# Decoder block: the operands of the down projection are made during gate/up and stored, and gate/up's products accumulate in PSUM

## The chip, the cores and the metric

One core of one Trainium2 chip. The metric is the device time of one execution in microseconds (us), less is better. All data is float32.

## The reference

One layer of a decoder trunk for 1024 tokens of width 1024. The part that matters here is the feed-forward block, with d_ff = 2816:

```python
x = x + merged @ w_out[i]
h = rms_norm(x, norm_ffn[i])
x = x + (jax.nn.silu(h @ w_ffn_gate[i]) * (h @ w_ffn_up[i])) @ w_ffn_down[i]
gate = jax.nn.sigmoid(rms_norm(x, norm_ple[i]) @ w_ple_gate[i])
```

Ahead of it come an input projection, a pooling mixer and an attention, after it an embedding gate and a final norm. None of those is changed.

## The kernel before

Features lie on the 128 partitions, tokens run along the free dimension. TensorE multiplies float32r operands, so each float32 operand is held as a pair hi + lo, made by `split`: ScalarE casts hi (L105), VectorE subtracts it for lo (L106). A product of two pairs takes three matmuls (`mm3`, L85 to L87), each 128x128 by 128x512.

Gate, up and down each use Strassen's scheme in Winograd's form: seven products in place of eight, for a pair of 128 outputs, two halves of the contracted features and two halves of the tokens. One such group is called a strassen here.

**Gate and up.** For each of 11 pairs of output tiles one strassen of gate and one of up run in turn (`strassen`). Each has 7 products of 12 matmuls, so 84. A product goes to a PSUM bank of its own (`bank`, eight of them, in turn). GpSimd sums the four weight pieces (L688 to L691), each weight operand is split, and the seven activation operands (`b11` to `t4`) have been made once ahead. Results are combined on VectorE: p1 is copied out by ScalarE (L682), and six adds from PSUM (`plus`, L674; one of p5 is used twice, so seven instructions) form the four outputs. Gate's outputs pass Silu (L712); up's are multiplied with them (L723) and written to DRAM (`d_a`, `flush`, L719), as plain float32. The order of each engine's instructions here is found by the framework's list scheduler, not by the program text; weight casts run three products ahead of TensorE (`bufs=4`).

**Down.** It runs over five chunks of four feature tiles and, in each, four pairs of output tiles (`mp`): 20 strassens of 7 products of 6 matmuls, 168 matmuls a chunk. The order is written by hand (`manual_schedule`). For the next chunk, `staged` loads eight activation tiles from `d_a` (L760), and `building` makes its 14 operands: 8 subtractions on GpSimd (L782, L788, L793, L798) and 14 splits, of which 12 subtract on VectorE and 2 on GpSimd (`LATE`). `prepare` makes the next strassen's weight operands (GpSimd L851 to L854, then splits: three of 512 columns, one of 256). `evacuate` adds each product from PSUM to a sum (L868 on ScalarE for 16 products of the first chunk, L870 on VectorE for the rest). In the last chunk nothing is built; `combine` forms x from the sums on GpSimd and VectorE (L879). The building of chunk 0 happens beside the last up strassen.

Operands lie in a ring of 48 tiles of 128x512 in three pools (`tap`, `tbp`, `spare`).

Of the kernel before, what the change touches and what calls it, by code (L numbers as in the profile page):

```python
# [16 lines left out]
P = 128  # L17
S = 1024
# [20 lines left out]
LATE = (("t3", 2), ("t4", 2))       # operands of down whose low parts GpSimd makes  # L39
# [6 lines left out]
def hybrid_block(ctx, tc, xT, pT, gains, pscale, w_u, w_qk, w_v, w_ga, w_gb, w_pool, w_a, w_b,  # L46
# [36 lines left out]
    def mm3(ps, w, x, first, last):  # L83
        """ps += (w_hi + w_lo)^T (x_hi + x_lo), less lo^T lo."""
        nc.tensor.matmul(ps, w[0], x[0], start=first, stop=False)  # L85
        nc.tensor.matmul(ps, w[0], x[1], start=False, stop=False)  # L86
        nc.tensor.matmul(ps, w[1], x[0], start=False, stop=last)  # L87
# [25 lines left out]
    def inv_rms(ps, acc, n, y):  # L113
        """y: [128 tokens, n], 1 / rms of n tiles of tokens; acc: sums of squares [features, n * 128]."""
        for t in range(n):
            nc.tensor.matmul(ps[:, t:t + 1], acc[:, t * P:(t + 1) * P], ones[:, :1], start=True, stop=True)
        a = const.tile([P, KT], F32, name="nrm_a", bufs=2)[:, :n]
        t = const.tile([P, KT], F32, name="nrm_t", bufs=2)[:, :n]
        nc.vector.tensor_scalar(a, ps[:, :n], EPS, None, ALU.add)
        # the first guess from the exponent's bits (within 4%), then Newton's steps  # L120
        nc.vector.tensor_scalar(y.bitcast(I32), a.bitcast(I32), -0.5, float(0x5f3759df), ALU.mult, ALU.add)
        for _ in range(3):
            nc.vector.tensor_mul(t, a, y)
            nc.vector.scalar_tensor_tensor(t, t, -0.5, y, ALU.mult, ALU.mult)
            nc.vector.scalar_tensor_tensor(y, t, 1.5, y, ALU.add, ALU.mult)
# [5 lines left out]
    def stat(psp, acc, n, diag):  # L131
        """diag: 1 / rms of n tiles of tokens, as diagonals side by side."""
# [5 lines left out]
    def spread(psp, diag, n):  # L138
        """[128, n * 128] in PSUM: the diagonals' entries along the free dimension, on all partitions."""
# [7 lines left out]
    def move(dst, src):  # L147
        """float32r as it is, through scratch in DRAM."""
# [28 lines left out]
    # x: load, times the norm's gain, split; the first three column tiles of u as x comes in  # L177
# [62 lines left out]
    def to_qk(pool, psp, i):  # L240
        """i < 4: q of a pair of heads; else k."""
# [17 lines left out]
    # pooling mixer  # L259
# [41 lines left out]
    # v: [keys, heads, 128]; hi|lo for even heads, lo|hi for odd ones  # L301
# [80 lines left out]
    with att, pool("att", 2) as ap, ExitStack() as pss:  # L382
# [5 lines left out]
        def scores(ld, qt):  # L388
            """The weights of 128 queries over the keys, [queries, keys]."""
# [31 lines left out]
        def turn(b, qt, ats):  # L421
            """[keys, queries], split; of a pair's two tiles, the second starts one block of keys later."""
# [23 lines left out]
        def att_out(h, hh, av):  # L446
            """hi part of v on the head's own half, lo part on the other."""
# [81 lines left out]
    # weights from here on, in pieces of 512 columns  # L529
# [23 lines left out]
    # [128, 512] operands: three pools, filled in turn, 16 + 24 + 8 tiles, as one ring  # L553
    def operand_tile(pool, dt=F32R):
        return pool.tile([P, HALF], dt, name="t")

    def operand(pool, n=4):
        return [(operand_tile(pool), operand_tile(pool)) for _ in range(n)]

    sparex = ctx.enter_context(ExitStack())  # L560
    spare = sparex.enter_context(pool("spare", 8, side="right"))
# [22 lines left out]
    tap = ctx.enter_context(pool("tap", 16))  # L584
# [75 lines left out]
    tbp = tbx.enter_context(pool("tbp", 24, side="right"))  # L660
    t2, t1, b22 = (operand(tbp) for _ in range(3))
    tb2x = ctx.enter_context(ExitStack())
    tb2 = tb2x.enter_context(pool("tb2", 16))
    t3, t4 = operand(tb2), operand(tb2)

    def product(a, b, k0=0):
        ps = bank()
        for k in range(len(b)):
            mm3(ps, col(a, k0 + k), b[k], k == 0, k == len(b) - 1)
        return ps  # L670

    def plus(ps, t, into=None):
        into = ev() if into is None else into
        nc.vector.tensor_add(into, ps, t)  # L674
        return into

    def strassen(src, out):
        """out(e, h, t): e-th tile of 128 outputs, half h of the tokens; a step is one product."""
        a11, a12, a21, a22 = (piece(src[e][:, hs(c)]) for e in range(2) for c in range(2))
        p1 = product(halves(a11), b11)  # L680
        t = ev()
        nc.scalar.copy(t, p1)  # L682
        yield
        p2 = product(halves(a12), b21)
        out(0, 0, plus(p2, t))
# [18 lines left out]
        yield  # L704
        p4 = product(halves(a22), t4)
        out(1, 0, plus(p4, t, t))
# [4 lines left out]
    def gate_out(e, h, t):  # L711
        nc.scalar.activation(t, t, AF.Silu)  # L712
# [4 lines left out]
    def flush(n):  # L717
        for _ in range(min(n, len(writes))):
            nc.sync.dma_start(*writes.pop(0))  # L719

    def up_out(i):
        def f(e, h, t):
            nc.vector.tensor_mul(t, t, gated.pop((e, h)))  # L723
            writes.append((d_a[2 * i + e][:, hs(h)], t))
        return f

# [25 lines left out]
    # down: the same products, over pairs of 128 outputs and four tiles of features at a time  # L752
    def staged(c, tile):
        """Activations of a chunk, k-th tiles of its halves: [k][y11, y12, y22, y21]."""
        ys = []
        for k in range(2):
            ys.append([])
            for f, h in ((k, 0), (k, 1), (2 + k, 1), (2 + k, 0)):
                ys[-1].append(tile())
                nc.sync.dma_start(ys[-1][-1], d_a[4 * c + f][:, hs(h)])  # L760
                yield ys

    ring = {"at": 0}

    def ring_pair():
        pair = []
        for _ in range(2):
            i = ring["at"] % 48
            ring["at"] += 1
            pair.append(operand_tile(tap if i < 16 else tbp if i < 40 else spare))  # L770
        return tuple(pair)

    def building(ys, o):
        """The chunk's operands in the order of the ring; a step is one of them, split."""
        for y in ys:
            o["b11"].append(ring_pair())
            split(*o["b11"][-1], y[0], teng("b11", len(o["b11"])))
            yield
        for y in ys:
            o["b21"].append(ring_pair())  # L780
            split(*o["b21"][-1], y[3], teng("b21", len(o["b21"])))
            nc.gpsimd.tensor_sub(y[0], y[1], y[0])  # L782
            yield
        t2s = [ring_pair() for _ in ys]
        for y in ys:
            o["t1"].append(ring_pair())
            split(*o["t1"][-1], y[0], teng("t1", len(o["t1"])))
            nc.gpsimd.tensor_sub(y[0], y[2], y[0])  # L788
            yield
        for y, t in zip(ys, t2s):  # L790
            o["t2"].append(t)
            split(*t, y[0], teng("t2", len(o["t2"])))
            nc.gpsimd.tensor_sub(y[1], y[2], y[1])  # L793
            yield
        for y in ys:
            o["b22"].append(ring_pair())
            split(*o["b22"][-1], y[2], teng("b22", len(o["b22"])))
            nc.gpsimd.tensor_sub(y[3], y[3], y[0])  # L798
            yield
        for n, i in (("t3", 1), ("t4", 3)):  # L800
            for y in ys:
                o[n].append(ring_pair())
                split(*o[n][-1], y[i], teng(n, len(o[n])))
                yield

    def operands():
        return {n: [] for n in ("b11", "b21", "t2", "t1", "b22", "t3", "t4")}

    def teng(n, k):
# [279 lines left out]
```

## Time and profile before

| what | value |
|---|---|
| runs | 1490.47, 1491.53, 2020.46 us; median 1491.53 |
| span of the profiled execution | 1489.5 us |
| TensorE busy | 1430.5 us, 96% |
| VectorE busy | 1075.6 us, 72% |
| ScalarE busy | 618.6 us, 42% |
| GpSimd busy | 479.8 us, 32% |
| DMA | 174.54 MB, mean 117 GB/s |

The profile is of one execution, whose own time outside the span is not listed; the two undisturbed runs lie 1.0 and 2.0 us above its span. A matmul's listed duration overlaps the next one's, so a matmul's cost is read from the distance between starts, or from a stretch's length over its count.

### The profile page before, as it was taken

To read this page: it belongs to the slowest core of one execution; us is meant where nothing else is said; L and a number is where in the kernel's file an instruction comes from. 1 tells how busy PE (TensorE), PEld (TensorE's weight loads), DVE (VectorE), ACT (ScalarE), POOL (GpSimd) and SP (SyncE) were. 2 spreads that over 40 slices of the span, in tenths; PEclk is the share of its full clock that TensorE was granted. 3 is DMA by queue.
4 is the path that set the end of the run, shared out by engine and by line. 5 is a ranking of instruction groups with operands and counts; after the bars stand their busy time and mean duration, and the time that the engine had idled before them with its cause. 6 is when DMAs were issued, how large, how long until landed. Compare 5 with 4: busy or idle time off the path is not lost.

```text
span 1489.5 us, 19114 instructions
## 1 busy us (share of the span) xinstructions
PE 1430.5 (96%) x6538; PEld 1172.3 (79%) x6538; DVE 1075.6 (72%) x1634; ACT 618.6 (42%) x1146; POOL 479.8 (32%) x501
## 2 busy tenths in 40 slices
PE   8999999999999999998999999999999999987995
PEld 7888888888888878886888888888877777765885
DVE  7671268888777786679655555555579899999786
ACT  6131455555555443446333333333335433325443
POOL 5000022333232200016323222232356676779001
PEclk9999999999999999999999999999999999998998
DMA  5140874555442187332332222222224333211452
GB/s 198 64 140 24 278 215 142 154 157 143 128 127 72 50 272 237 114 119 87 117 121 86 79 83 80 80 83 73 84 64 135 114 99 113 71 43 57 134 178 70
DMA packets 94032, 174.54 MB, mean 117 GB/s; under 512 B 9968, under 2 KB 21744, under 8 KB 93936
## 3 DMA queue, kind: packets, MB, share of 16 engines
q1 hardware_dynamic: 93936, 173.33, 36.7%
q8 instruction: 51, 0.84, 0.2%
q14 instruction: 45, 0.37, 0.1%
HBM read 128.21 MB, written 45.09 MB: 116 GB/s over the span
## 4 chain that ended last, share of the span: by engine, by line
PE 74%; DVE 11%; issue 8%; POOL 4%; ACT 1%; DMA 1%; SPq 0%; POOLq 0%; DVEq 0%; ACTq 0%
PE mm L87 23%; PE mm L86 23%; PE mm L85 23%; DVE wlo L106 2%; DVE t L106 2%; DVE fail L410 1%; PE pt L428 1%; DVE xsl L110 1%; PE av L444 1%; PE av L443 1%; PE z L400 1%; PE z L401 1%; POOL x L879 1%; DVE s L870 1%; DVE x L957 1%
## 5 line engine op out<-in xcount | busy, mean ns | idle before, releaser
L105 ACT CAST whi<-wraw 128x512 fp32r<-128x512 f32 x336 | 206.2, 621 | 488.9 <-PE mm L86 357.0
L87 PE MATMUL mm<-t,wlo 128*128 128x512 f32 x960 | 381.2, 397 | 12.1 <-DVE wlo L106 12.0
L85 PE MATMUL mm<-t,whi 128*128 128x512 f32 x960 | 380.5, 397 | 12.0 <-ACT whi L105 8.3
L86 PE MATMUL mm<-t,whi 128*128 128x512 f32 x960 | 379.4, 395 | 1.2 <-DVE t L106 1.2
L106 DVE TENSOR_TENSOR wlo<-wraw,whi 128x512 fp32r<-128x512 f32 x336 | 264.4, 792 | 124.1 <-ACT whi L105 124.1
L87 PEld LDWEIGHTS mm<-t,wlo 128*128 128x128 f32 x960 | 181.9, 189 | 61.0 <-DVE wlo L106 20.7
L85 PEld LDWEIGHTS mm<-t,whi 128*128 128x128 f32 x960 | 181.9, 190 | 55.9 <-ACT whi L105 10.6
L86 PEld LDWEIGHTS mm<-t,whi 128*128 128x128 f32 x960 | 181.7, 189 | 43.4 <-DVE t L106 2.2
L674 DVE TENSOR_TENSOR ev<-mm,ev 128x512 f32<-128x512 f32 x154 | 106.0, 689 | 128.3 <-PE mm L87 126.6
L85 PE MATMUL mm<-xs,whi 128*128 128x512 f32 x384 | 154.6, 403 | 0.0
L87 PE MATMUL mm<-xs,wlo 128*128 128x512 f32 x384 | 150.4, 392 | 0.0
L86 PE MATMUL mm<-xs,whi 128*128 128x512 f32 x384 | 150.2, 391 | 0.0
L688 POOL TENSOR_TENSOR ws<-wraw 128x512 f32<-128x512 f32 x22 | 30.7, 1397 | 329.5 <-DMA wraw<-in_w_gate 224.2
L410 DVE TENSOR_TENSOR_SCAN fail<-fail 128x1024 f32<-128x1024 f32 (+3 forms) x64 | 87.3, 1364 | 27.3 <-POOL fail L408 26.8
L408 POOL TENSOR_SCALAR_AFFINE_SELECT fail<-fail 128x128 f32<-128x128 f32 x64 | 20.5, 320 | 227.0 <-ACT fail L406 200.5
L87 PEld LDWEIGHTS mm<-xs,wlo 128*128 128x128 f32 x384 | 72.1, 188 | 15.8
L105 ACT CAST ath<-pt 128x256 fp32r<-128x256 f32 (+1 forms) x176 | 54.8, 335 | 69.0 <-PE pt L428 38.9
L85 PEld LDWEIGHTS mm<-xs,whi 128*128 128x128 f32 x384 | 72.2, 188 | 11.9 <-ACT sg L372 0.2
L86 PEld LDWEIGHTS mm<-xs,whi 128*128 128x128 f32 x384 | 72.4, 188 | 11.5
L106 DVE TENSOR_TENSOR t<-ev,t 128x512 fp32r<-128x512 f32 x76 | 78.3, 1043 | 0.4
L106 DVE TENSOR_TENSOR atl<-pt,ath 128x256 fp32r<-128x256 f32 (+1 forms) x176 | 61.4, 367 | 18.2 <-ACT ath L105 17.9
L409 POOL TENSOR_SCALAR_AFFINE_SELECT beta<-beta 128x128 f32<-128x128 f32 x64 | 66.5, 1038 | 22.6 <-ACT beta L407 21.0
(191 smaller groups left out, 2608.2 us busy)
## 6 DMA issues: line engine op xcount, KB each, us to landing
wraw<-in_w_gate SPq DMA_DIRECT2D x44, 256.0 KB, 2.6
wraw<-in_w_up SPq DMA_DIRECT2D x44, 256.0 KB, 2.6
d_a<-ev SPq DMA_DIRECT2D x44, 256.0 KB, 2.0
wraw<-in_w_down SPq DMA_DIRECT2D x44, 256.0 KB, 2.7
ev<-d_a SPq DMA_DIRECT2D x36, 256.0 KB, 4.3
wraw<-in_w_out SPq DMA_DIRECT2D x32, 256.0 KB, 3.1
wraw<-in_w_pg SPq DMA_DIRECT2D x32, 256.0 KB, 2.6
wraw<-in_w_qk SPq DMA_DIRECT2D x8, 512.0 KB, 4.6
```

What stands on the lines that cost most here:

```text
L85: nc.tensor.matmul(ps, w[0], x[0], start=first, stop=False)
L86: nc.tensor.matmul(ps, w[0], x[1], start=False, stop=False)
L87: nc.tensor.matmul(ps, w[1], x[0], start=False, stop=last)
L105: nc.scalar.copy(hi, src)
L106: (eng or nc.vector).tensor_sub(lo, src, hi)
L110: nc.vector.scalar_tensor_tensor(lo, src, g, hi, ALU.mult, ALU.subtract)
L400: nc.tensor.matmul(zo, q[:, base:base + P], kh[:, ks], start=True, stop=False)
L408: nc.gpsimd.affine_select(r[:, :P], r[:, :P], [[1, P]], ALU.is_gt, 1.0, base=0, channel_multiplier=-1)
L409: nc.gpsimd.affine_select(b[:, :P], b[:, :P], [[1, P]], ALU.is_gt, 0.0, base=0, channel_multiplier=-1)
L410: nc.vector.tensor_tensor_scan(r[:, :w], r[:, :w], r[:, :w], 1.0, ALU.mult, ALU.bypass)
L674: nc.vector.tensor_add(into, ps, t)
L688: nc.gpsimd.tensor_add(s1, a21, a22)
```

## The change

Gate/up: p1, p6, p7 and p4 of a strassen now accumulate in one PSUM bank (`x`) and p5 and p3 in a second one (`y`); p2 has its own. Between two products on the same bank its content is read: ScalarE copies p1, p1+p6 (`u2`) and p5 out (three copies in place of one), and VectorE adds for three outputs (three adds in place of seven). The fourth output needs no add. p7 and p3 change places.

After each up strassen (but the last) its four outputs stay in SBUF. `stage` makes from them the seven operands of down during the next gate strassen: 7 splits (ScalarE and VectorE) and 4 subtractions on GpSimd, one step behind each product. Each operand, hi and lo side by side in one 128x1024 tile of `spare`, is written to DRAM (`d_o`, 512 KB each, 70 in all), on the same queue as the weight loads.

Down: `staged` and `building` are gone. `loading` fetches 14 operands of 512 KB per chunk, straight into the ring (now 24 tiles of 128x1024); chunk 0's are fetched during the last up strassen. To pair the tiles rightly, `prepare` takes even and odd feature tiles as the two halves, so its operands are strided views. Matmuls, evacuations and `combine` stay as they were.

```diff
-    d_a = [scr(f"d_a{i}", [P, S]) for i in range(FT)]
+    d_o = [{n: scr(f"d_{n}{i}", [P, S]) for n in DOWN} for i in range(FT // 2 - 1)]
...
+        def kept(ps):
+            t = ev()
+            nc.scalar.copy(t, ps)
+            return t
+
+        x = product(halves(a11), b11)
+        p1 = kept(x)
+        yield
+        out(0, 0, product(halves(a12), b21), p1)
         yield
...
-        p6 = product(halves(a11), t2)
-        plus(p6, t, t)
-        yield
-        p5 = product(halves(s1), t1)
-        c12 = plus(p5, t)
-        yield
-        p3 = product(halves(a12), b22)
-        out(0, 1, plus(p3, c12, c12))
-        yield
-        p7 = product(halves(a21), t3)
-        plus(p7, t, t)
-        out(1, 1, plus(p5, t))
-        yield
-        p4 = product(halves(a22), t4)
-        out(1, 0, plus(p4, t, t))
+        product(halves(a11), t2, ps=x)
+        u2 = kept(x)
+        yield
+        y = product(halves(s1), t1)
+        p5 = kept(y)
+        yield
+        product(halves(a21), t3, ps=x)
+        out(1, 1, x, p5)
+        yield
+        product(halves(a12), b22, ps=y)
+        out(0, 1, y, u2)
+        yield
+        product(halves(a22), t4, ps=x)
+        out(1, 0, x, None)
         yield
...
+    def store(dst, src):
+        t = pair_tile(spare)
+        split(*sides(t), src)
+        writes.append((dst, t))
+
+    def stage(i, ys):
+        d = d_o[i]
+        store(d["b11"], ys[0, 0])
+        nc.gpsimd.tensor_sub(ys[0, 0], ys[0, 1], ys[0, 0])
+        yield
+        store(d["b22"], ys[1, 1])
+        yield
+        store(d["b21"], ys[1, 0])
+        yield
+        store(d["t1"], ys[0, 0])
+        nc.gpsimd.tensor_sub(ys[0, 0], ys[1, 1], ys[0, 0])
+        nc.gpsimd.tensor_sub(ys[0, 1], ys[1, 1], ys[0, 1])
+        yield
+        store(d["t2"], ys[0, 0])
+        nc.gpsimd.tensor_sub(ys[1, 0], ys[1, 0], ys[0, 0])
+        yield
+        store(d["t3"], ys[0, 1])
+        yield
+        store(d["t4"], ys[1, 0])
+        yield
...
+    def loading(c, o):
+        for n in DOWN:
+            o[n] = []
+            for k in range(2):
+                t = ring_pair()
+                move(t, d_o[2 * c + k][n])
+                o[n].append(sides(t))
+                yield
...
+        for _ in g:
+            next(staging, None)
+            flush(1)
+        run(staging)
...
-        a11, a12, a21, a22 = x[:, :q], x[:, q:], y[:, :q], y[:, q:]
+        (a11, a12), (a21, a22) = ([t.rearrange("p (k e d) -> p e k d", e=2, d=P)[:, e] for e in range(2)] for t in xy)
...
-                    if (mp, n) >= (1, 2) and (mp < 3 or n > 1):
-                        next(build, None)
...
+                if n % 2 == 1 and mp < 3 or mp == 3 and n >= 1:
+                    next(ops, None)
```

## Rows read from the trace of the kernel before

**Rows 1.** Stretches: length; PE, PEld, DVE, ACT, POOL busy (count); clock; DMA; GB/s.

```profile
540.00:570.00 30.00, 30.00 (x134) 24.86 (x133) 26.23 (x42) 9.03 (x16) 0.00 (x0) 1.00 0.81 271
740.00:1100.00 360.00, 360.00 (x1564) 293.12 (x1563) 207.96 (x297) 113.07 (x186) 105.38 (x76) 1.00 0.26 85
1104.00:1131.00 27.00, 24.60 (x104) 18.89 (x103) 25.55 (x29) 11.90 (x23) 21.35 (x15) 1.00 0.24 79
1131.00:1295.00 164.00, 153.46 (x642) 121.05 (x641) 149.72 (x201) 68.26 (x129) 114.15 (x102) 0.98 0.33 104
1295.00:1346.00 51.00, 45.03 (x188) 35.64 (x187) 51.00 (x66) 12.24 (x23) 39.23 (x31) 0.97 0.21 64
```

**Rows 2.** Waits, 1104 to 1346 us: waiter, releaser, total us, times, longest.

```profile
ACT whi L105 <- POOL wraw L854: 66.1, 17, 5.4
...
POOL wraw L853 <- DVE wlo L106: 22.2, 15, 3.6
POOL ev L788 <- DVE t L106: 19.6, 8, 4.6
```

**Rows 3.** The same view, TensorE's waits alone.

```profile
PE mm L87 <- DVE wlo L106: 10.4, 11, 3.7
PE mm L85 <- ACT whi L105: 8.3, 4, 2.4
```

**Rows 4.** Timeline of one stall in down: start, duration, engine, [idle before, releaser].

```profile
1278.65 1.75 POOL L793 TENSOR_TENSOR ev<-ev 128x512 f32<-128x512 f32 x1
...
1284.01 0.72 POOL L854 TENSOR_TENSOR wraw<-wraw 128x256 f32<-128x256 f32 x1
...
1284.76 0.62 ACT L105 CAST whi<-wraw 128x512 fp32r<-128x512 f32 x1 [4.38 <-POOL wraw L854]
...
1285.43 0.50 PE L85 MATMUL mm<-t,whi 128*128 128x512 f32 x1 [2.26 <-ACT whi L105]
...
1288.11 0.63 PE L85 MATMUL mm<-t,whi 128*128 128x512 f32 x1
...
1288.53 0.63 PE L86 MATMUL mm<-t,whi 128*128 128x512 f32 x1
```

**Rows 5.** Durations of lo splits, ns min/median/max: gate/up first, then down.

```profile
L106 DVE TENSOR_TENSOR wlo<-wraw,whi x112: 681/684/1686, 741.8 to 1098.7; 128x512 fp32r<-128x512 f32 x112
...
L106 DVE TENSOR_TENSOR wlo<-wraw,whi x46: 674/693/1791, 1130.9 to 1292.4; 128x512 fp32r<-128x512 f32 x46
L106 DVE TENSOR_TENSOR wlo<-ws,whi x15: 409/416/1509, 1134.6 to 1286.4; 128x256 fp32r<-128x256 f32 x15
```

**Rows 6.** GpSimd durations by line, ns min/median/max.

```profile
L690 POOL TENSOR_TENSOR wraw<-ws,wraw x22: 1290/1296/1297, 660.1 to 1094.0; 128x512 f32<-128x512 f32 x22
...
L854 POOL TENSOR_TENSOR wraw<-wraw x20: 722/740/1722, 1122.9 to 1324.0; 128x256 f32<-128x256 f32 x20
```

**Rows 7.** DMA issues: KB each, median us to landing.

```profile
hv<-d_v SPq DMA_DIRECT2D x8, 512.0 KB, 4.3
```

**Rows 8.** Waits in steady gate/up, 740 to 1100 us.

```profile
POOL ws L688 <- DMA wraw<-in_w_up: 83.9, 9, 9.4
```

**Rows 9.** Groups in 740 to 1100 us: count, busy us, mean ns, idle before.

```profile
L674 DVE TENSOR_TENSOR ev<-mm,ev 128x512 f32<-128x512 f32 x131 | 90.4, 690 | 121.2 <-PE mm L87 119.5 <-DMA d_a<-ev 1.7
...
L105 ACT CAST whi<-wraw 128x512 fp32r<-128x512 f32 x112 | 69.7, 622 | 203.6 <-PE mm L86 202.1 <-PE mm L87 1.5
...
L682 ACT COPY ev<-mm 128x512 f32<-128x512 f32 x18 | 10.4, 580 | 0.0
```

**Rows 10.** Timeline in steady gate/up, where p1 of a strassen ends.

```profile
871.51 0.40 PE L87 MATMUL mm<-t,wlo 128*128 128x512 f32 x1
871.60 0.58 ACT L682 COPY ev<-mm 128x512 f32<-128x512 f32 x1
...
871.75 0.39 PE L85 MATMUL mm<-t,whi 128*128 128x512 f32 x1
```

**Rows 11.** Timeline in the last up strassen, ScalarE.

```profile
1116.38 0.62 ACT L105 CAST t<-t 128x512 fp32r<-128x512 f32 x1 [2.75 <-POOL t L788]
```

More of the change, by code (lines that the diff above doesn't have):

```diff
@@ L38 @@
 NRAW = 6
-LATE = (("t3", 2), ("t4", 2))
+DOWN = ("b11", "b21", "t2", "t1", "b22", "t3", "t4")
 @with_exitstack
@@ L81, in weight, with mm3 @@
         return hi, lo
[L83 to L87, printed above, removed]
+    def mm3(ps, w, x, first, last, onto=False):
+        nc.tensor.matmul(ps, w[0], x[0], start=first, stop=False, skip_group_check=onto)
+        nc.tensor.matmul(ps, w[0], x[1], start=False, stop=False, skip_group_check=onto)
+        nc.tensor.matmul(ps, w[1], x[0], start=False, stop=last, skip_group_check=onto)
     def col(w, k):
@@ L159, in hybrid_block @@
     d_e = [scr(f"d_e{i}", [P, S]) for i in range(KT)]
-    d_a = [scr(f"d_a{i}", [P, S]) for i in range(FT)]
+    d_o = [{n: scr(f"d_{n}{i}", [P, S]) for n in DOWN} for i in range(FT // 2 - 1)]
+    d_l = [[scr(f"d_l{e}{h}", [P, HALF]) for h in range(2)] for e in range(2)]
     icol = const.tile([P, KT], F32, name="icol")
@@ L659, in hybrid_block, with product @@
     tbx = ctx.enter_context(ExitStack())
-    tbp = tbx.enter_context(pool("tbp", 24, side="right"))
+    tbp = tbx.enter_context(pool("tbp", 12, side="right"))
     t2, t1, b22 = (operand(tbp) for _ in range(3))
     tb2x = ctx.enter_context(ExitStack())
-    tb2 = tb2x.enter_context(pool("tb2", 16))
+    tb2 = tb2x.enter_context(pool("tb2", 8))
     t3, t4 = operand(tb2), operand(tb2)
[L666 to L669, printed above, removed]
-        return ps
[L672 to L675, printed above, removed]
+    def product(a, b, cols=range(4), ps=None):
+        first = ps is None
+        ps = bank() if first else ps
+        for k, x in enumerate(b):
+            mm3(ps, col(a, cols[k]), x, first and k == 0, k == len(b) - 1, not first)
+        return ps
     def strassen(src, out):
         a11, a12, a21, a22 = (piece(src[e][:, hs(c)]) for e in range(2) for c in range(2))
-        p1 = product(halves(a11), b11)
-        t = ev()
-        nc.scalar.copy(t, p1)
+        def kept(ps):
[4 more added lines that the diff above has]
+        p1 = kept(x)
         yield
-        p2 = product(halves(a12), b21)
-        out(0, 0, plus(p2, t))
+        out(0, 0, product(halves(a12), b21), p1)
         yield
@@ L750, in hybrid_block @@
     embed(16)
[L753 to L771, printed above, removed]
@@ L806, in operands, with ring_pair @@
-    def operands():
-        return {n: [] for n in ("b11", "b21", "t2", "t1", "b22", "t3", "t4")}
-    def teng(n, k):
-        return nc.gpsimd if (n, k) in LATE else nc.vector
     NF = FT // 2
     NC = FT // 4
+    ring = {"at": 20}
+    def ring_pair():
+        i = ring["at"] % 24
+        ring["at"] += 1
+        return pair_tile(tap if i < 8 else tbp if i < 20 else spare)
+    def loading(c, o):
[6 more added lines that the diff above has]
+                yield
@@ L814, in hybrid_block @@
+    staging = iter(())
+    op = {}
     for i in range(NF):
         g = strassen([w_gate[2 * i], w_gate[2 * i + 1]], gate_out) if i else first
-        for n, _ in enumerate(g):
-            if n == 1:
-                flush(2)
-        if i == 2:
-            *_, ys = staged(0, lambda: operand_tile(spare, F32))
-        if i == NF - 1:
-            op = operands()
-            build = building(ys, op)
-        for n, _ in enumerate(strassen([w_up[2 * i], w_up[2 * i + 1]], up_out(i))):
-            if n in (4, 5):
-                flush(1)
-            if i == NF - 1 and n > 0:
-                next(build)
-                next(build)
@@ L830, in hybrid_block @@
-    flush(2)
+        for _ in g:
+            next(staging, None)
+            flush(1)
+        run(staging)
+        flush(len(writes))
+        if i == NF - 1:
+            ops = loading(0, op)
+            for _ in range(4):
+                next(ops)
+        ys = {}
+        for n, _ in enumerate(strassen([w_up[2 * i], w_up[2 * i + 1]], up_out(ys))):
+            if i == NF - 1 and n in (2, 3, 4, 5, 6):
+                next(ops)
+                next(ops)
+        if i < NF - 1:
+            staging = stage(i, ys)
+        else:
+            for (e, h), t in ys.items():
+                nc.sync.dma_start(d_l[e][h], t)
@@ L888, in hybrid_block @@
             if mp == 0:
-                nxt = operands()
+                nxt = {}
+                ops = loading(c + 1, nxt) if c < NC - 1 else iter(())
                 if c == NC - 1:
@@ L893, in hybrid_block @@
                 ahead = prepare(raws.pop(i + 1))
-            for n, name in enumerate(("b11", "b21", "t2", "t1", "b22", "t3", "t4")):
+            for n, name in enumerate(DOWN):
                 if n == 0 and i + 2 < len(order):
@@ L928, in hybrid_block @@
             if c < NC - 1 and mp == 3:
-                for _ in build:
-                    pass
+                run(ops)
                 op = nxt
```

103 lines of the change are left out of this document (40 added, 63 removed).

## The prediction

> **What bounds the kernel now.** I read stretches first, then waits, then one stall. In steady gate/up, 740 to 1100 us, TensorE is busy for all of 360 us and does 1564 matmuls [rows 1]: 360 / 1564 = 0.230 us each, and the waits of TensorE list nothing there. This is the floor of a matmul in this kernel; nothing that relieves another engine can speed this stretch. VectorE is at 208 / 360 = 58%, ScalarE at 31%, GpSimd at 29%.
>
> From the last up strassen on it is different. Length less count times 0.230 gives what TensorE lost: 27.0 - 104 x 0.230 = 3.1 us in 1104 to 1131, 164.0 - 642 x 0.230 = 16.3 us in chunks 0 to 3 of down, and 51.0 - 188 x 0.230 = 7.8 us in the last chunk and its end [rows 1]. Together 27.2 us, 1.8% of 1489.5. That is all the change can win.
>
> Who is late there? ScalarE's weight casts wait 66.1 us for GpSimd's L854, GpSimd waits 22.2 and 19.6 us for VectorE's splits [rows 2], and TensorE ends up waiting for lo and hi of weights, the latter four times, once per chunk [rows 3]. One stall shows the chain: GpSimd does a subtraction of `building` in 1.75 us, is done with L854 at 1284.73, the cast starts at 1284.76 after 4.38 us of waiting, TensorE at 1285.43 after 2.26 us idle; and then its matmuls start 0.42 us apart (1288.11, 1288.53), at half the clock [rows 4].
>
> Why are both late? A lo split takes 0.68 us at its least and up to 1.79 [rows 5]; GpSimd's sums take 1.30 us on 512 columns and 0.74 on 256, up to 1.72 [rows 6]. The long ones lie where the two engines overlap. If such instructions (both inputs in SBUF) simply take turns, a chunk of down costs, at their short durations: VectorE 12 operand splits and 12 weight splits x 0.68 = 16.3, 4 x 0.41 = 1.6; GpSimd 8 subtractions and 2 splits x 1.30 = 13.0, 16 x 0.74 = 11.8: 42.7 us. TensorE needs 168 x 0.230 = 38.6. The four chunks ran at 164 / (642 / 168) = 42.9 us each [rows 1]. So I take the turns of VectorE and GpSimd as what paces down.
>
> The Trainium skill's page "SBUF — State Buffer", section "Terms", calls the port pair of the two engines exclusive, held for a whole instruction, with the other fully blocked. By that rule turns are the whole story; the 42.9 us agree with it.
>
> **The change, part by part.**
>
> *Down, chunks 0 to 3.* The 14 operand splits and 8 subtractions go. What takes turns is then 12 x 0.68 + 1.6 + 11.8 = 21.6 us of 38.6, and VectorE in all 28 evacuations x 0.68 = 19.0 more, 28.8 us. TensorE becomes the bound. I take 15 of the 16.3 us as won and leave 1.3 for the start of the first chunk. `prepare`'s views become strided, 2 x 128 columns in place of 256; no row shows this. It costs between 0 and the price of 512 columns, 1.30 - 0.74 = 0.56 us x 16 = 9 us a chunk; even then 30.6 of 38.6. I take 0.
>
> *Last up strassen.* Building chunk 0 there is gone: 3.1 us won.
>
> *Last chunk.* Nothing was built in it. Its turns: weights of three strassens 9 x 0.68 + 3 x 0.41 + 12 x 0.74 = 16.2, four activation splits 2.7, `combine` three times 3 x 0.68 + 5 x 1.30 = 25.6; 44.5 us against 38.6. These stay, so 5.9 of the 7.8 us stay and 2 are won (4 if VectorE, now with no backlog at the start, absorbs more).
>
> Sum so far: 15 + 3 + 2 = 20 us won.
>
> *Loads of down.* 14 x 0.52 MB = 7.3 MB of operands and 2.1 MB of weights a chunk, over 38.6 us: 244 GB/s, before 104. In 540 to 570 us the DMA engines moved 271 GB/s at a share of 0.81 while TensorE did 134 matmuls in 30 us, its full rate [rows 1]. A 512 KB load lands in 4.3 us [rows 7], and each is issued at least eight products, 11 us, before its use. A load into the ring must wait for the tile's last reader, the chunk's b11 or b21 at worst, and the weight loads queue behind it on SP; they are two strassens, 19 us, ahead. Cost 0; if the cover fails, one late 4.3 us landing per chunk, 17 us in four.
>
> *Stores of gate/up.* 7 x 0.52 MB a pair, with weights 5.8 MB in 38.6 us, 150 GB/s, under the same 271. On SP each store waits for its split, and the weight loads of the next strassen stand behind it. GpSimd already waits 9 us at a time for such loads [rows 8] and TensorE does not feel it, because casts run three products (8.3 us) ahead. Cost 0; up to one store's wait of 1 or 2 us is inside that cover.
>
> *Staging, work moved to gate.* Per pair: 7 casts, 7 lo splits, 4 subtractions, all in the gate half. By its shares above, a pair (38.6 us) has 22.3 us of VectorE, 12.1 of ScalarE, 11.3 of GpSimd. VectorE loses eight adds at 0.69 [rows 9] and gains seven splits: 22.3 - 5.5 + 4.8 = 21.6. ScalarE: 12.1 + 7 x 0.62 + 4 x 0.58 = 18.8 [rows 9]. GpSimd: 11.3 + 4 x 1.30 = 16.5. Averages are fine. Turns are less fine: the gate half (19.3 us) has 14 splits x 0.68 + 8 x 1.30 = 19.9 us, the up half 11 x 0.68 + 4 x 1.30 = 12.7. Gate is full, up has room, the pair takes 32.6 of 38.6.
>
> *The new waits.* p6, p7 and p4 may not start before the bank `x` has been read, nor p3 before `y`. Queued behind each such matmul is all of TensorE. Today the copy of p1 starts 0.09 us after p1's last matmul begins and ends at 872.18, while the next product runs from 871.75 to 874.51 [rows 10]: 2.3 us to spare, so nothing is lost if ScalarE is free. For the output add on VectorE after p7 (0.69) it is 2.2. What can spoil it is order: both engines run in order, and a staging cast that waits for a GpSimd subtraction holds the copy behind it. In the last up strassen, where `building` did twice the staging work per strassen, ScalarE stood 2.75 us for such a subtraction [rows 11]. If one such wait begins just as a product ends, the copy is done 2.75 + 0.62 + 0.58 = 3.95 us later, 1.2 us too late; if it began 1.2 us earlier, nothing is lost. No row shows these waits with the new order, so between 0 and four casts x 1.2 = 4.8 us per gate strassen. I take 0.5, near the low end: the nearest row, the last up strassen, lost 3.1 us with twice the load. Ten gate strassens are staged beside: 5 us lost.
>
> A copy costs what L682 does, 0.58 [rows 9]. Matmuls that add to a full bank should take 0.230 as those inside a product do. The first gate strassen, short of operands, saves at most two adds, 1.4 us; I leave it at 0.
>
> *Total.* Span 1489.5 - 20 + 5 = 1474.5; the median run lies 2.0 above the span, so 1476.5.
>
> **Rivals.**
>
> *All clean.* The scheduler places the copies well and the last chunk gives 4: 1491.5 - 15 - 3 - 4 = 1469.5; with every lost microsecond back, 1464.3. For it: ScalarE at 50%. Against: the full gate half.
>
> *The gain is eaten.* By the rule of turns the gate half is 0.6 us over its 19.3. VectorE then runs late by more than the 2.2 us it may at p7's add, and TensorE waits about 2 us a gate strassen: 20 us, 1491.5. For it: 19.9 against 19.3. Against: the up half can take the overhang, and weight splits have 8 us of cover.
>
> The same sentence of the Trainium skill ("SBUF — State Buffer", "Terms") is the rule behind this rival.
>
> *Slower.* ScalarE's queue meets the worst case at all four GpSimd-fed casts: 4.8 us, and stops that long bring the half clock, as after the 2.26 us stall: eight matmuls 0.2 us longer each, 1.6 us. 6.4 x 10 = 64 us, 1535. It decides from 2.0 us per gate strassen (slower than before), and from 5.0 it is over 2%. Against: it needs bad luck at every cast.
>
> *Down isn't relieved.* The change takes operands away but the weights' GpSimd sums are what ScalarE waits for; if they are late by themselves (strided views, loads), the 15 us stay: 1491.5 - 5 + 5 = 1491.5. Against: 21.6 of 38.6.
>
> **How the numbers follow.** Forecast 0.52, clean 0.16, eaten 0.19, slower 0.07, not relieved 0.06. The range goes from 1464 (all 27.2 us back) to 1497 (eaten, with half a microsecond more a strassen); it leaves out slower and little else. Two per cent, about what a measurement of this kernel can tell from no change, is 29.8 us, more than all that was lost: over 2% faster needs a faster matmul as well, 0.03. Over 2% slower is the slower rival, 0.07. The rest, 0.90, is within.
>
> **What would show it.** In the changed profile: down's matmul count times 0.230 near its length in the first four chunks, with no ScalarE wait for L854 of this size; stalls only in the last chunk; VectorE under 80% in down, still full at its end; DMA near 240 GB/s in down and 150 in gate/up. In gate/up a new list of TensorE waits for ScalarE's copies or VectorE's adds, in gate halves only: 5 us in all if I am right, 20 if eaten. I am wrong if these exceed 20 us, if TensorE waits for operands from DRAM, or if the matmul's 0.230 moves.

## The result, and the profile after

Four runs of the changed kernel gave a median of 1479.79 us (1479.62 to 1483.41), the kernel before on the same chip 1490.47 to 1493.87, with one disturbed run of 2020.46 us that the comparison leaves out. The ratio is 0.9928, 95% interval 0.9913 to 0.9943: 0.7% faster, which is within two per cent. The profiled span is 1477.6 us against 1489.5: 11.9 us less. The forecast was 1476.5 us for the median, 15 us less.

The table follows TensorE: each stretch runs from the start of one matmul to the start of another, the same two in both traces.

| stretch | before | after | change | forecast |
|---|---|---|---|---|
| up to the 24th matmul of the first gate strassen | 688.4 | 688.0 | -0.4 | 0 |
| from there to the end of the first pair (144 matmuls) | 44.3 | 49.8 | +5.5 | 0 |
| pairs 2 to 10 and the last gate strassen | 368.0 | 368.5 | +0.5 | +5 |
| last up strassen | 21.7 | 24.3 | +2.6 | -3 |
| down, chunks 0 to 3 | 172.4 | 154.0 | -18.4 | -15 |
| down, last chunk | 41.4 | 39.4 | -2.0 | -2, with the next row |
| the last two feature tiles, up to the first matmul behind down | 27.9 | 28.6 | +0.7 | (above) |
| from there to the last matmul | 117.6 | 117.1 | -0.5 | 0 |

So the sum came out 3 us off, from four terms that were each off by 3 to 6 and partly cancel. Stretches after the change (length; PE, PEld, DVE, ACT, POOL busy and count; clock; DMA share; GB/s):

```profile
740.00:1100.00 360.00, 360.00 (x1562) 291.99 (x1561) 227.79 (x289) 164.24 (x290) 157.08 (x111) 1.00 0.43 152
1106.00:1131.00 25.00, 21.80 (x89) 17.34 (x88) 10.00 (x15) 7.04 (x13) 8.83 (x8) 0.93 0.71 270
1131.00:1284.00 153.00, 153.00 (x669) 125.36 (x668) 96.78 (x159) 44.03 (x80) 48.94 (x66) 1.00 0.70 254
1284.00:1324.00 40.00, 39.60 (x172) 31.81 (x171) 38.09 (x49) 11.29 (x21) 26.92 (x23) 1.00 0.27 89
1324.00:1353.00 29.00, 25.28 (x100) 20.05 (x99) 28.61 (x32) 12.58 (x22) 27.16 (x17) 0.88 0.23 73
```

They answer to [rows 1]. In down's first four chunks TensorE is now busy for all 153 us and runs 669 matmuls, 0.229 us each: nothing is lost there. DMA moves 254 GB/s, forecast 244; in gate/up it is 152, forecast 150. VectorE falls to 63% in down and stays at 38.09 of 40 us in the last chunk. Where time went instead is in two places.

The first pair. TensorE's waits from 660 to 740 us, first before, then after (waiter, releaser, total us, times, longest):

```profile
PE mm L85 <- ACT t L105: 1.3, 2, 0.9
PE mm L86 <- DVE t L106: 1.2, 1, 1.2
```

```profile
PE mm L85 <- ACT t L105: 4.4, 3, 1.8
PE mm L86 <- DVE t L106: 3.8, 2, 2.5
```

`t` are the activation operands, which are still being split there. TensorE waits at the same two lines in both, and longer after the change.

The last up strassen. Its timeline after the change, the SP queue's issues first:

```profile
1097.73 3.09 SPq L149 DMA_DIRECT2D t<-d_b  x4
1100.87 0.67 SPq L535 DMA_DIRECT2D wraw<-in_w_up  x1
...
1108.96 1.30 POOL L694 TENSOR_TENSOR ws<-wraw 128x512 f32<-128x512 f32 x1 [14.64 <-DMA wraw<-in_w_up]
1111.70 1.27 POOL L696 TENSOR_TENSOR wraw<-ws,wraw 128x512 f32<-128x512 f32 x1
1113.00 0.62 ACT L105 CAST whi<-wraw 128x512 fp32r<-128x512 f32 x1 [5.98 <-POOL wraw L696]
...
1114.57 0.58 ACT L685 COPY ev<-mm 128x512 f32<-128x512 f32 x1
1115.20 0.80 PE L85 MATMUL mm<-t,whi 128*128 128x512 f32 x1 [3.20 <-ACT ev L685]
```

Read from the bottom: TensorE waits 3.20 us for the copy of p1, as the second product on that bank must. The copy is queued on ScalarE behind casts of weights, the first of which waited 5.98 us for GpSimd's sums. GpSimd in turn waited 14.64 us for a weight load, which SP issued behind four loads of down's operands. It landed some 8 us after its issue.

### The profile page after: what moved, and what is told of

Read it like the earlier page. It is cut to its first block, busy times and chain, and to the rows that moved or that the text cites. A ratio compares the mean times of both kernels' runs of the same rounds, so it can differ in the third digit from the quotient of the medians.

```text
span 1477.6 us, 19192 instructions
## 1 busy us (share of the span) xinstructions
PE 1425.9 (96%) x6538; PEld 1171.9 (79%) x6538; DVE 1018.9 (69%) x1556; ACT 640.4 (43%) x1190; POOL 450.6 (30%) x491
## 4 chain that ended last, share of the span: by engine, by line
PE 80%; DVE 10%; issue 6%; POOL 1%; DMA 1%; ACT 1%; SPq 0%; POOLq 0%; DVEq 0%; ACTq 0%
PE mm L87 25%; PE mm L86 25%; PE mm L85 25%; DVE wlo L106 2%; DVE fail L411 1%; PE pt L429 1%; DVE t L106 1%; DVE xsl L110 1%; PE av L445 1%; PE av L444 1%; PE z L401 1%; PE z L402 1%; DVE ev L606 1%; DVE x L956 1%; PE mm L141 1%
## 5 line engine op out<-in xcount | busy, mean ns | idle before, releaser
L106 DVE TENSOR_TENSOR wlo<-wraw,whi 128x512 fp32r<-128x512 f32 x336 | 253.6, 760 | 188.1 <-ACT whi L105 181.3
L106 DVE TENSOR_TENSOR t<-ev,t 128x512 fp32r<-128x512 f32 x98 | 96.9, 1010 | 32.9 <-ACT t L105 32.6
L105 ACT CAST t<-ev 128x512 fp32r<-128x512 f32 x102 | 61.6, 620 | 82.0 <-DVE ev L739 37.7
L105 ACT CAST ath<-pt 128x256 fp32r<-128x256 f32 (+1 forms) x176 | 54.8, 335 | 69.5 <-PE pt L429 38.8
```

Source lines behind the costliest of these rows:

```text
L105: nc.scalar.copy(hi, src)
L106: (eng or nc.vector).tensor_sub(lo, src, hi)
```

## The experiments

**The loads of chunk 0 behind the weight loads**, in the changed kernel.

```diff
             ops = loading(0, op)
-            for _ in range(4):
-                next(ops)
...
-            if i == NF - 1 and n in (2, 3, 4, 5, 6):
+            if i == NF - 1:
                 next(ops)
                 next(ops)
```

> Change: chunk 0's first four operand loads are issued beside the first two products of the last up strassen, behind its weight loads, in place of ahead of them. Theory: the 3.2 us stop in the last up strassen (and 1.6 us at half the clock behind it) stands because four 512 KB loads are ahead of up's weight loads on the DMA queue, so GpSimd gets the last weight piece late, ScalarE's casts wait and hold the copy of p1 behind them. It expects the stop to go, the last up strassen to take 19.3 to 20 us in place of 24.3, and 4 to 5 us less than the changed kernel (about 1475). Rival: the copy of p1 between products is late by itself (the PSUM dependency); then the stop stays and the time is that of the changed kernel, 1479.8 within 1.

Measured: 1473.38 us (1472.68 to 1474.77), ratio to before 0.9867 (0.9842 to 0.9892), span 1472.8. The last up strassen takes 19.4 us:

```profile
1098.00:1131.00 33.00, 33.00 (x145) 26.74 (x144) 15.08 (x23) 12.02 (x22) 10.74 (x11) 1.00 0.92 335
```

No idle time of TensorE is left there, and four loads of 512 KB in SP's queue ahead of a weight load cost 24.3 - 19.4 = 4.9 us. The two strassens by which the prediction had weight loads ahead hold in down, not here.

**The first gate strassen without accumulation**, with a bank per product and seven adds as before, once in the new order of products, once in the old.

```diff
-    first = strassen([w_gate[0], w_gate[1]], gate_out)
+    first = strassen_plain([w_gate[0], w_gate[1]], gate_plain, True)
```

`strassen_plain` is the old `strassen`; with True, p7 stands ahead of p3, with False behind it.

> Change: the first gate strassen alone uses a PSUM bank for each product and seven adds on VectorE again, with the new order of products (p7 ahead of p3). Theory A: the 5.5 us that the first gate strassen lost come from its products being tied to one bank, so that TensorE can't go on with another product while an operand is missing; expected: 4 to 5.5 us less than the changed kernel, about 1475. Theory B: they come from the order, t3 being wanted before b22; expected: no change, 1479.8 within 1, and the old order alone would bring it back. If VectorE is what counts there, four more adds cost up to 2.7 us: about 1482.

> Change: as the kernel with plain banks in the first gate strassen, but with the old order of products (p3 ahead of p7); the first gate strassen is then what it was before the change. All theories expect the 5.5 us back if they lie in this strassen at all, about 1474.5. Theory A (banks) expects the same as with the new order; theory B (order) expects this one alone to be faster. If neither is faster, the loss comes from somewhere ahead of it.

Measured: 1474.91 us (1473.04 to 1479.35), ratio 0.9882 (0.9847 to 0.9917), and 1476.02 (1473.22 to 1479.26), ratio 0.9884 (0.9854 to 0.9914). Both spans are 1472.7 us. From the 24th matmul to the end of the pair both take 44.3 us, as before the change. The order is worth nothing, the shared bank 5.5 us. The stretch 688 to 712 us in the kernel before, the changed one and the first of these two shows how much less TensorE gets done:

```profile
688.00:712.00 24.00, 17.67 (x58) 11.62 (x57) 24.00 (x27) 14.11 (x24) 17.42 (x13) 0.86 0.26 87
```

```profile
688.00:712.00 24.00, 13.65 (x34) 7.79 (x33) 22.05 (x23) 13.44 (x24) 17.64 (x12) 0.72 0.26 87
```

```profile
688.00:712.00 24.00, 17.81 (x58) 11.39 (x57) 24.00 (x26) 13.23 (x24) 17.46 (x13) 0.86 0.26 88
```

58 matmuls and 34. That the bank does it is shown; how is my reading: with a bank of its own, a product whose operands are there can begin while another one waits for its last operand, and on the shared bank it can't.

**No accumulation anywhere** (the plain form in all 22 strassens).

```diff
-        g = strassen([w_gate[2 * i], w_gate[2 * i + 1]], gate_out) if i else first
+        g = strassen_plain([w_gate[2 * i], w_gate[2 * i + 1]], gate_plain, True) if i else first
...
-        for n, _ in enumerate(strassen([w_up[2 * i], w_up[2 * i + 1]], up_out(ys))):
+        for n, _ in enumerate(strassen_plain([w_up[2 * i], w_up[2 * i + 1]], up_plain(ys), True)):
```

> Change: no accumulation in PSUM at all; every product of gate and up has a bank of its own and VectorE makes seven adds per strassen, while the operands of down are still made during gate, stored and loaded. Theory (turns of VectorE and GpSimd pace; adds from PSUM don't take turns; casts run three products ahead): steady gate/up still loses nothing, since a gate half is 19.9 us of turns either way and VectorE's 26 us a pair fit in 38.6; with the first strassen's 5.5 us back, about 1474 to 1476. Rival: the accumulation was needed to make room on VectorE; then each gate half stops 1 us or more, 10 us or more in ten, 1485 or more.

Measured: 1473.97 us (1471.22 to 1478.05), ratio 0.9872 (0.9841 to 0.9902), span 1476.1. Steady gate/up is the same (360 us for 1563 matmuls); VectorE does 278.1 us there in place of 227.8 and TensorE doesn't feel it. The time is that of the run with one plain strassen (1474.91), so accumulation buys nothing in this kernel: the four adds that it saves a strassen lie beside TensorE. The stop in the last up strassen stays:

```profile
PE mm L85 <- ACT whi L105: 2.8, 1, 2.8
```

Now TensorE waits directly for the cast of the late weights. The copy only passed the lateness on.

**Accumulation alone**, in the kernel before.

```diff
-        p6 = product(halves(a11), t2)
-        plus(p6, t, t)
+        product(halves(a11), t2, ps=x)
+        u2 = kept(x)
...
```

The other products change as in the change itself; `building` and `staged` stay.

> Change: to the kernel before, only the accumulation in PSUM banks is added (three copies, three adds, p7 ahead of p3); d_a, staging and building stay as they were. Theory: accumulation gives nothing in steady gate/up, which TensorE bounds anyway, and costs about 5.5 us in the first gate strassen; about 1496.5, with the down projection as slow as before. Rival: relieving VectorE of eight adds a pair pays somewhere (the backlog of the last up strassen, which also builds chunk 0); then 1491 or less.

Measured: 1502.03 us (1501.58 to 1504.98), ratio 1.0078 (1.0060 to 1.0097), span 1500.1, more than expected. The first pair loses 6.1 us by the stretches of the table. Another 5.1 are lost in the last up strassen, where `building` shares ScalarE with the copies:

```profile
PE mm L84 <- ACT ev L679: 5.7, 1, 5.7
```

This is the mechanism of the rival that was called slower, at one place in the kernel and not at ten.

**More GpSimd work in down**: the changed kernel with 8, then 16 adds on 512 columns a chunk that nothing uses.

```diff
+                if c < NC - 1 and n in (2, 3, 4, 6):
+                    nc.gpsimd.tensor_add(dum[0], dum[0], dum[1])
```

This is the edit for 16; for 8 a chunk, `n in (3, 4)`.

> Change: to the changed kernel, GpSimd gets two additions on 128x512 tiles in SBUF per strassen of down, 8 a chunk in the first four chunks (they compute nothing that is used; the kernel before had 8 subtractions there). Theory of turns (instructions of VectorE and GpSimd with two SBUF inputs don't overlap): 21.6 + 8 x 1.30 = 32.0 us of turns a chunk, under TensorE's 38.6, so nothing is lost, chunks at 38.1 to 38.8 us as now. Rival (each engine is limited by its own work only): the same. Only if GpSimd's place in the chain of weights counts will chunks be longer.

> Change: as the kernel with 8 additions, but four per strassen, 16 a chunk. Theory of turns: 21.6 + 16 x 1.30 = 42.4 us a chunk, so the chunks of down go at 42 to 43 us in place of 38.5 and the time rises by 14 to 17 us, to 1494 to 1497. Rival (own work only): GpSimd has 11.8 + 20.8 = 32.6 us and VectorE 28.8 of 38.6; nothing is lost, 1480.

Measured: one run each, 1483.02 and 1482.74 us, spans 1480.9 and 1480.4. Chunks 0 to 3 take 38.8, 38.1, 38.7, 38.4 us with 8 and the same with 16, as without. The 3 us more lie behind down, where nothing was edited. VectorE and GpSimd with 16 adds, two chunks (groups: count, busy us, mean ns, idle before):

```profile
L106 DVE TENSOR_TENSOR wlo<-wraw,whi 128x512 fp32r<-128x512 f32 x24 | 23.0, 958 | 9.0 <-ACT whi L105 8.4
L884 DVE TENSOR_TENSOR s<-mm,s 128x512 f32<-128x512 f32 x32 | 21.1, 680 | 0.0
...
L106 DVE TENSOR_TENSOR wlo<-ws,whi 128x256 fp32r<-128x256 f32 x8 | 12.1, 1508 | 0.0
```

```profile
L916 POOL TENSOR_TENSOR ev<-ev 128x512 f32<-128x512 f32 x32 | 47.2, 1476 | 1.9
L865 POOL TENSOR_TENSOR wraw<-wraw 128x256 f32<-128x256 f32 x8 | 8.8, 1105 | 0.6
```

At their short durations the two-input instructions of these 76 us come to 24 x 0.69 + 8 x 0.41 on VectorE [rows 5] and 32 x 1.30 + 32 x 0.74 on GpSimd [rows 6]: 85 us. They fit into 76 without TensorE losing anything. That the two engines take turns and the sum of the turns is the pace is refuted: 42.7 against 42.9 in the prediction was a coincidence.

**The chain of `building` cut**, in the kernel before. My next theory was that old down was paced by its chain of subtraction, cast, split, subtraction. The edit keeps every instruction and its place, but no split waits for a subtraction any more, so t1, t2, t3 and t4 are no longer the right sums.

```diff
-            split(*o["t1"][-1], y[0], teng("t1", len(o["t1"])))
+            split(*o["t1"][-1], y[1], teng("t1", len(o["t1"])))
...
-            split(*t, y[0], teng("t2", len(o["t2"])))
-            nc.gpsimd.tensor_sub(y[1], y[2], y[1])
+            split(*t, y[2], teng("t2", len(o["t2"])))
+            nc.gpsimd.tensor_sub(y[0], y[2], y[0])
...
-            nc.gpsimd.tensor_sub(y[3], y[3], y[0])
+            nc.gpsimd.tensor_sub(y[0], y[3], y[0])
```

> The kernel before with the same number of casts, splits and GpSimd subtractions at the same places of down, but none of building's operands waits for a subtraction any more: each split reads a loaded tile, and the four subtractions all write one tile that only they and b11's split touch, so t1, t2, t3 and t4 are not the right sums. Theory now (the chain subtraction, cast, split, subtraction, in queues that the weights share, paces the old down): chunks 0 to 3 fall from 42.9 to about 38.7 us, span about 1475, 15 us less than before. Rival (the amount of VectorE and GpSimd work paces it, by turns or otherwise): chunks stay at 42 to 43 us, span about 1489.

Measured: 1493.56 us (1492.08 to 1497.6), ratio 1.0022 (1.0012 to 1.0031), span 1491.0. Chunks take 42.2, 44.6, 44.7, 44.6 us, so the chain isn't what it takes to make them slow, and that theory falls too. Yet the cut changes what TensorE waits for. Its waits over the last two of the four chunks, in the kernel before and then with the chain cut:

```profile
PE mm L85 <- ACT whi L105: 4.7, 2, 2.4
PE mm L87 <- DVE wlo L106: 0.6, 2, 0.4
```

```profile
PE mm L87 <- DVE wlo L106: 8.4, 2, 4.3
```

In the kernel before, the stop of [rows 4] ends with a cast that waited for GpSimd's L854. GpSimd was late there because it had stood 4.57 us for a split of VectorE, and VectorE in the end idled itself:

```profile
1275.08 1.29 POOL L788 TENSOR_TENSOR ev<-ev 128x512 f32<-128x512 f32 x1 [4.57 <-DVE t L106]
...
1285.41 1.09 DVE L106 TENSOR_TENSOR wlo<-wraw,whi 128x512 fp32r<-128x512 f32 x1 [2.06 <-ACT whi L105]
```

With the chain cut, TensorE waits for VectorE's own splits, and longer.

**The old work without its chain**, in the changed kernel: in chunks 0 to 3 the same casts, splits and subtractions at the same places, on scratch tiles that nothing uses.

```diff
...
+                if c < NC - 1 and (mp, n) >= (1, 2) and (mp < 3 or n > 1) and made < 14:
+                    hi, lo = dhi[made % 3], dlo[made % 2]
+                    nc.scalar.copy(hi, dsrc)
+                    (nc.gpsimd if made in (11, 13) else nc.vector).tensor_sub(lo, dsrc, hi)
+                    if 2 <= made < 10:
+                        nc.gpsimd.tensor_sub(dsub, dsrc, dsub)
+                    made += 1
```

> The changed kernel, plus in each of chunks 0 to 3 of down the old building's amount of work at the old building's places: 14 casts, 14 lo subtractions (12 on VectorE, 2 on GpSimd) and 8 GpSimd subtractions, all on scratch tiles that nothing uses, so without the chain. Theory (the chain paces the old down): chunks stay at about 38.5 us, at most 39.5, span 1477 to 1481. Rival (the amount of work): 42 to 43 us a chunk, span about 1494.

Measured: span 1499.2 us, one run at 1501.07. Chunks take 40.6, 44.1, 44.3, 44.2 us: the old work is enough to bring the old times back. It isn't quite free of chains: the casts have three tiles in turn, so each waits until the split of the third cast before it has read its tile, and ScalarE stands 33.6 us in 23 such waits from 1125 to 1340 us. VectorE over two chunks (88 us), then the same in the kernel before (87 us) and in the changed one (77 us):

```profile
L924 DVE TENSOR_TENSOR ev<-ev 128x512 f32<-128x512 f32 x24 | 23.9, 994 | 0.0
L106 DVE TENSOR_TENSOR wlo<-wraw,whi 128x512 fp32r<-128x512 f32 x24 | 23.2, 967 | 4.0 <-ACT whi L105 4.0
L885 DVE TENSOR_TENSOR s<-mm,s 128x512 f32<-128x512 f32 x32 | 21.4, 679 | 0.0
L885 DVE TENSOR_TENSOR x<-mm,x 128x512 f32<-128x512 f32 x24 | 16.3, 678 | 0.0
L106 DVE TENSOR_TENSOR wlo<-ws,whi 128x256 fp32r<-128x256 f32 x8 | 7.7, 960 | 0.0
```

```profile
L106 DVE TENSOR_TENSOR t<-ev,t 128x512 fp32r<-128x512 f32 x24 | 25.4, 1058 | 0.0
L870 DVE TENSOR_TENSOR s<-mm,s 128x512 f32<-128x512 f32 x33 | 22.0, 677 | 0.0
L106 DVE TENSOR_TENSOR wlo<-wraw,whi 128x512 fp32r<-128x512 f32 x25 | 21.2, 847 | 5.1 <-ACT whi L105 5.1
L870 DVE TENSOR_TENSOR x<-mm,x 128x512 f32<-128x512 f32 x25 | 16.9, 676 | 0.0
L106 DVE TENSOR_TENSOR wlo<-ws,whi 128x256 fp32r<-128x256 f32 x8 | 5.5, 685 | 0.0
```

```profile
L880 DVE TENSOR_TENSOR s<-mm,s 128x512 f32<-128x512 f32 x32 | 21.2, 682 | 0.0
L106 DVE TENSOR_TENSOR wlo<-wraw,whi 128x512 fp32r<-128x512 f32 x24 | 16.6, 693 | 22.5 <-ACT whi L105 22.4
L880 DVE TENSOR_TENSOR x<-mm,x 128x512 f32<-128x512 f32 x24 | 16.4, 682 | 0.0
L106 DVE TENSOR_TENSOR wlo<-ws,whi 128x256 fp32r<-128x256 f32 x8 | 3.4, 426 | 1.1 <-ACT whi L105 0.6
```

Listed durations add up to 92.5 us in 88, 91.0 in 87, and 57.6 in 77 (neighbours overlap a little); with 16 dummy adds, 72.5 in 76. VectorE idles 4 or 5 us in the two slow kernels, 9 with 16 dummy adds and 24 in the changed one. Note that the adds that read PSUM keep 0.68 us in all four; only the splits, with both inputs in SBUF, get longer when GpSimd works beside them.

Over a whole chunk VectorE isn't always full where time is lost: chunks 0 and 1 of the kernel before take 42.7 us with VectorE busy 88% of it, as much as in the chunks with 16 dummy adds (87 to 89% in chunks 1 to 3), which lose nothing. A strassen at a time shows more. This is the last of the four chunks, each strassen from its first matmul to the next one's: length in us, share in which VectorE is busy.

| kernel | 1st | 2nd | 3rd | 4th |
|---|---|---|---|---|
| before | 9.8, 100% | 9.7, 94% | 9.7, 100% | 14.5, 86% |
| before, chain cut | 9.7, 94% | 9.7, 85% | 9.7, 100% | 15.6, 100% |
| changed, old work without its chain | 9.6, 95% | 9.6, 85% | 9.6, 100% | 15.4, 100% |
| changed, 16 dummy adds | 9.6, 87% | 9.6, 88% | 9.6, 88% | 9.6, 88% |
| changed | 9.6, 70% | 9.6, 70% | 9.6, 70% | 9.6, 70% |

So old down had no slow pace. It had one long stop a chunk, at the third product of the fourth strassen, after a third strassen in which VectorE had no idle time. The fourth strassens of chunks 0 to 3 took 12.6, 13.7, 14.1 and 14.5 us before the change, 16.3 us more than 4 x 42 x 0.230; all four chunks lost 18.0.

Chunk 0 separates two causes in part. There ScalarE takes 16 of the 28 evacuations, and VectorE's work in the third strassen is, at short durations, 3 adds, 9 splits of 512 columns and one of 256: 12 x 0.68 + 0.41 = 8.6 us for 9.7. Even so, with the old work unchained VectorE is busy without a break in the third and fourth strassen of chunk 0, and TensorE stops for 1.5 us. Its splits in that chunk (1130 to 1170 us) are long:

```profile
L924 DVE TENSOR_TENSOR ev<-ev 128x512 f32<-128x512 f32 x12 | 12.9, 1090 | 0.2 <-ACT ev L923 0.2
L106 DVE TENSOR_TENSOR wlo<-wraw,whi 128x512 fp32r<-128x512 f32 x10 | 11.0, 1104 | 7.0 <-ACT whi L105 7.0
```

This speaks for the lengthening beside GpSimd as a part of the cause. It doesn't prove it, since VectorE had also idled 7.0 us for weight casts, some of which stand behind the dummy casts.

**No `combine` in the last chunk** (the changed kernel; three pairs of x are not final).

```diff
-                        if n == 0:
-                            comb = combine(mp - 1)
-                        next(comb, None)
+                        pass
```

> The changed kernel without combine for the first three pairs of output tiles in the last chunk, so that these three pairs of x are not final. Theory of the prediction's last-chunk step (combine's adds on GpSimd and VectorE are what VectorE is late with there): the stop of 3.7 us after the last chunk and the half clock behind it go, together about 6 us, span 1471.5. Rival (the stop comes from the splits of the last two feature tiles and of the weights themselves): it stays, span 1477 or more.

Measured: one run of 1468.94 us, span 1466.8, more won than expected. The last chunk takes 38.4 us, the two feature tiles behind it 22.4 in place of 28.6, and VectorE is busy 30.3 of 38.4 us. Before the edit TensorE's waits from 1283 to 1350 us are

```profile
PE mm L87 <- DVE wlo L106: 4.1, 2, 3.7
```

and with it none. The 6.2 us are the stop and what follows it: 10 matmuls run 0.427 us apart, at a granted clock of 0.50, the 1.2 GHz level. Another 2.7 us won lie in a later stop for a lo split, 7.0 us long in place of 9.7.

**Both repairs together**: late loads and a plain first gate strassen in the new order; then the same with five of `combine`'s eight adds on VectorE in place of three. The edit shown is that of the second.

```diff
-            (nc.vector if i in (1, 3, 5) and mp < KT // 2 - 1 else nc.gpsimd).tensor_add(*o)
+            (nc.vector if i in (1, 3, 5, 6, 7) and mp < KT // 2 - 1 else nc.gpsimd).tensor_add(*o)
```

> Change: the two mends together: chunk 0's first operand loads behind the last up strassen's weight loads, and the first gate strassen with a bank for each product. The losses lie 400 us apart, so the gains should add: 1479.8 - 4.7 - 5.5 = 1469.6; 1468 to 1471. If the time is above 1472, one of them was in part given back later.

> The faster combination (plain first gate strassen, first operand loads of down behind the last up weights' loads) with five in place of three of combine's eight adds on VectorE. If GpSimd's long adds hold the last chunk, the stop behind it shrinks and the run takes 2 to 5 us less than the combination, about 1468; if VectorE's own queue holds it, two more adds of 0.68 us per pair make it later: up to 4 us more, about 1475.

Measured: both repairs 1471.6 us (1466.86 to 1472.21), ratio 0.9861 (0.9841 to 0.9881), span 1469.9. The last chunk ends 11.1 us earlier than in the changed kernel (5.5 and 4.9 were to be had), but the last stretch of the table takes 120.1 us in place of 117.1, with no edit there. With the adds moved 1471.43 (1469.97 to 1474.25), ratio 0.9875 (0.9858 to 0.9891): the two times can't be told apart. The traces tell more. TensorE's waits from 1275 to 1400 us, with both repairs and then with the adds moved as well:

```profile
PE mm L87 <- DVE wlo L106: 13.5, 3, 9.3
```

```profile
PE mm L87 <- DVE wlo L106: 9.6, 3, 6.8
PE mm L116 <- POOL acc L599: 3.4, 1, 3.4
```

The stop behind the last chunk grows from 3.7 to 6.8 us, as expected if VectorE's own queue holds it, and the later stops shrink by as much in all, so that the time stays.

## Why the prediction was right, and where its steps were not

The verdict and the range held, and down's relief is real. That the time came within 3 us is in part luck: two steps came out 5 to 6 us worse than forecast (the first pair, the last up strassen) and two others 3 to 5 us better. By its own steps:

- *"So I take the turns of VectorE and GpSimd as what paces down."* This step failed, though the time it gave was near. The runs with dummy adds refute the sum of turns. The step also took one stop a chunk for an even pace. What the runs show instead is a VectorE that falls behind in the second and third strassen, where 11 of its 12 operand splits are queued, and the stop that follows: the sum left out VectorE's adds from PSUM, 28 a chunk in chunks 1 to 3. By an estimate from the short durations, the third strassen of these chunks gives VectorE 16 x 0.68 + 0.41 = 11.3 us of work for 9.7, the whole chunk 24 x 0.68 + 1.6 + 28 x 0.68 = 37 for 38.6, and beside GpSimd its splits list 7 to 9 us a chunk more (before (24 x 0.37 + 25 x 0.15 + 8 x 0.26) / 2 = 7.4, with the old work unchained (24 x 0.30 + 24 x 0.27 + 8 x 0.53) / 2 = 9.0, against the means of the changed kernel). The prediction had the 19.0 us of evacuations at hand, but used them for the kernel after alone.
- *Down, 15 us won.* Mis-sized: 18.4. The 1.3 us left for the start of the first chunk weren't needed, and the four chunks had lost more than 16.3 us counted from matmul to matmul (172.4 less 4 x 38.6 is 18.0). Strided views cost nothing that shows: GpSimd's sums on 256 columns keep a median of 0.74 us.
- *Last up strassen, 3.1 us won.* Failed: 2.6 lost. The cost lay in *"the weight loads queue behind it on SP ... Cost 0"*: the argument was made for down's ring, and the same loads at the start of chunk 0 stand ahead of a load that the running strassen needs. Moving them gives back 4.9 us, so the strassen ends 2.3 us shorter than before the change, near the forecast.
- *First gate strassen, "I leave it at 0."* Failed: 5.5 lost, all from the shared bank. The step counted instructions and not, as I read it, the freedom to run ahead that was lost.
- *Ten gate strassens, 5 us lost.* Mis-sized: 0.5 for pairs 2 to 10 and the last gate together; no wait of TensorE is listed from 740 to 1100 us. The 2.2 us of room behind p1 and p7 were enough there. The list scheduler kept the copies timely, as in the rival *all clean*, and VectorE was at 63%, ScalarE at 46%, GpSimd at 44%, near the 56, 49 and 43 that the staging sum gave.
- *Last chunk, 2 us won of 7.8.* Chunk and feature tiles together won 1.3. The cause given, `combine`, holds: without it the stop and the half clock go. Why it costs is, as far as the runs show, again VectorE: it is busy 38.1 of 40 us, and two more adds a pair on it make the stop 3.1 us longer.
- *The gain is eaten* had the gate half over its 19.3 us by the rule of turns; no loss came. The Trainium skill, "SBUF — State Buffer", section "Terms", has the loser of the port pair fully blocked for a whole instruction. The traces agree that both engines get slower, but not with a sum of whole durations: 85 us fitted into 76. Its section "SBUF: two separate sides" names, as VectorE's part in this, instructions in a two-port mode or with two SBUF inputs. The trace agrees as far as it goes: the adds with one input in PSUM stayed at 0.68 us.

Not run: VectorE's 12 operand splits alone, without GpSimd's part. So it is shown that GpSimd's amount by itself doesn't slow a chunk, that the chain isn't needed, and that in chunks 0 to 3 the long stops come behind a strassen in which VectorE never idled. How much of its lateness is VectorE's own work and how much the lengthening beside GpSimd stays open.

## What to carry to other kernels

Add up everything that is queued on an engine, step by step, and hold each sum against its step, before you explain a late engine by how it shares or waits. A mean over a stretch hides a single stop in it. A sum that fits one number may still be the wrong one, and a dummy load on the suspected engine tells in one run. When a step is moved to another time, look at what its DMAs stand ahead of in the queue at that time. A shared accumulator was free where the next product's operands were ready, and cost 5.5 us where they came one by one.

## What the runs showed of the hardware

- A stop of TensorE can cost more than its length. After idling 3.7 us behind the last chunk, 10 matmuls ran 0.427 us apart (granted clock 0.50, the 1.2 GHz level) where the steady distance is 0.230, 2.0 us more; the stop of 3.2 us in the last up strassen was followed by 6 such. It doesn't always: in the kernel before, the stop of 2.4 us in chunk 1 was followed by none (granted clock 1.00 from 1199.3 to 1203 us), that of 2.4 us in chunk 2 by several (0.66 from 1242 to 1247).
- VectorE's instructions with both inputs in SBUF went from 693 to 958 ns on 512 columns and from 426 to 1508 on 256 on average when GpSimd was kept busy (95% of the time); those that read PSUM stayed at 680.
- With no stop, 168 matmuls of a chunk took 38.8, 38.1, 38.7 and 38.4 us, the same to 0.1 us in the changed kernel and nine of its variants. Why chunk 1 is quicker wasn't tried.
